# A two-layer encoder trunk: the last group of w_down, too, by seven block products

## The chip, the cores and the metric

The kernel runs on one core of a Trainium2 chip. The metric is the device time of one execution in microseconds (us). Before the change it is 2019.84 us, the median of 3 runs (2019.82 to 2021.61). One execution was recorded by the hardware profiler; its own time is 2019.96 us.

A core has a matrix engine (TensorE, PE in the profile, its weight loads PEld), a vector engine (VectorE, DVE), a scalar engine (ScalarE, ACT), GpSimd (POOL) and SyncE (SP), which issues nearly all loads here. Each engine runs its own list of instructions in order and waits on semaphores for the others.

## The reference

Two layers over 256 tokens of width 2048, all in float32. Each layer is a normalisation, a mixing part (three kinds of attention and an output projection), another normalisation and a feed-forward part that is 8192 wide. The change touches only the second product of the feed-forward part:

```python
h = rmsnorm(x, norm_mlp[l])
u = jax.nn.relu(jnp.einsum('bsd,df->bsf', h, w_up[l]))
x = x + jnp.einsum('bsf,fd->bsd', u * u, w_down[l])
...
return rmsnorm(x, norm_final)
```

## The kernel before

**Precision.** Every float32 operand of a matmul is kept as two parts in a shorter format: a high part (`whi`, a ScalarE cast) and the rest (`wlo`, a VectorE subtraction, `TENSOR_TENSOR` on L989). The helper `split` (L978) makes both for one weight tile of 128x1024. A product takes three matmuls instead of one: high by high, low by high and high by low. The activations `uT` carry both parts from the start.

**Steps.** The program is a list of steps (`steps`), one weight tile each. While step i runs, loads are issued for six steps ahead (L964), the split of step i + 2 is made and preparations of step i + 4 (`prep`). The tiles whi and wlo rotate through three buffers each, so the split of a step waits until the step three places ahead of it has used its own. A scheduler turns this list into an order for each engine.

**The feed-forward part** is cut into eight groups g of 1024 hidden columns. Group g has 16 *up steps* (`up_steps`, L691 and L696: 8 matmuls of 512 columns and 8 of 256), which make four tiles uT of 256 hidden columns each, and it has its share of w_down, 1024 rows by 2048 columns. The four column chunks j of 512 are taken in two ways:

- *Plain steps* (`down_steps`, matmuls on L477): for a chunk, 4 steps of 12 matmuls add up in two PSUM banks, one for each half of the tokens, and VectorE adds the banks to the residual x (L739).
- *Product steps* (`strassen_steps`, L802): chunks 0 and 1 of groups 0 to 6 are seen as 2x2 block matrices and computed with seven block products instead of eight. They go by the names P1, P6, P7, P5, P3, P2, P4, in this order. A product is two steps (h = 0 and 1) of 6 matmuls. The weight sums that the products need (B12 + B11 and so on) are made by VectorE over 128x1024 (`prep`, L815 to L832); the sums of activation blocks are made once for each uT tile (`sums_of`, L712 to L717). P1, P6, P5 and P3 add up in one bank, P7 and P4 in a second one, both in the tile S; P2 has its own. Behind each product VectorE adds the bank to x (L782). The next product that writes S waits for that.

The quarters of w_down are B11, B12, B22 and B21, each in two halves. B11 lies in the tiles `spare`, the others in `side`, of which there are four; B21's halves come last and take the places of B12's, once P7's splits have read those.

**The order** is written out by hand. With group g's products go group g's plain steps for chunks 2 and 3 and the up steps of group g + 1:

```python
for g in range(7):
    ss = down_steps(g, (2, 3)) + up_steps(g + 1)
    hs = strassen_steps(g)
    order = [0, 0]
    for p_ in range(7):
        order += [1, 0, 1] + ([0, 0] + [0] * (p_ in (1, 3, 5)) if p_ < 6 else [])
steps.extend(down_steps(7, range(4)))
```

A 1 is a product step, a 0 the next of the others. Between two products stand two or three other steps. Group 7 is four plain chunks, 16 steps, and behind each chunk `layer_end` starts the next layer's transposes of that chunk (`hprep`), or in the last layer the squares for the final normalisation (`final_chunk`).

Of the kernel before, what the change touches and what calls it, by code (L numbers as in the profile page):

```python
# [23 lines left out]
P = 128  # L24
# [19 lines left out]
def tile_trunk(ctx: ExitStack, tc: tile.TileContext, x_in, w_in, w_o, w_up, w_down,  # L44
# [459 lines left out]
    def layer_steps(l):  # L504
# [152 lines left out]
        def up_steps(g):  # L657

            out_, evacs = [], []
            for q in range(4 * g, 4 * g + 4):  # L660
                box = {}

                def evac(q=q, box=box):
# [14 lines left out]
                    if q < 28:  # L678
                        sums_of(q, a)
# [40 lines left out]
        def down_steps(g, js):  # L720
            out_ = []
            for j in js:
                box = {}
                for k in range(4):
                    def mm(wh, wl, j=j, k=k, box=box):
                        if k == 0:
                            box["b"] = [mm_bank(), mm_bank()]
                            box["w"] = []
                        final = l == L - 1 and g == 7 and j == 3
                        hts = [uT[4 * g + k]] * 2  # L730
                        mode_b(box["b"], hts, wh, wl, [0, 1], k == 0, k == 3, blocks=(0,) if final else (0, 1),
                               lo_last=g < 7)
                        box["w"].append((hts, wh, wl))
                        if k < 3:
                            return

                        def evac(t):
                            xs = x[:, t, j * 512:(j + 1) * 512]
                            nc.vector.tensor_add(xs, xs, box["b"][t])  # L739
                        if final:  # L740
                            evac(0)
                            final_block(0)
                            tail = [mm_bank(), mm_bank()]
                            for c in range(2):
                                cols = slice(c * 256, c * 256 + 256)
                                for i, (hts, vh, vl) in enumerate(box["w"]):
                                    mode_b([None, tail[c]], hts, vh[:, :, cols], vl[:, :, cols], [0, 1],
                                           i == 0, i == 3, n=256, blocks=(1,))
                                xs = x[:, 1, 1536 + c * 256:1792 + c * 256]
                                nc.vector.tensor_add(xs, xs, tail[c][:, 0:256])  # L750
                                square_cols(1, 1536 + c * 256, 256, fin["ss"][:, 7 + c:8 + c])
                            final_block(1)
                            return
# [421 lines left out]
```

## Time and profile before

| | |
|---|---|
| median of 3 runs | 2019.84 us |
| profiled execution, its own time | 2019.96 us |
| its span, first to last instruction | 2018.2 us |
| TensorE busy | 2003.0 us (99%) |
| VectorE busy | 1644.0 us (81%) |
| ScalarE busy | 1208.2 us (60%) |
| group 6 of the second layer | about 1880.8 to 1966.3 us |
| group 7 of the second layer, plain | 1966.3 us to the end of its matmuls |

Rows of the timeline give start, length, engine, line, operation, the tile written and the tiles read, the shape and a count; a bracket at the end is the engine's idle time before the row and what ended it. A matmul's length overlaps the next one, so times are taken from start to start. Rows of windows give a stretch, its length and each engine's busy time.

### The profile page before, as it was taken

The numbers are of one execution on the slowest core, as the hardware profiler recorded it, in microseconds if no ns is written. First come the engines' busy times: TensorE is split into PE (matmuls) and PEld (weight loads), VectorE is DVE, ScalarE is ACT, GpSimd is POOL, SyncE is SP. The second block draws the span as 40 slices with busy tenths as digits, with TensorE's granted clock in tenths as the row PEclk, the third lists the DMA queues.
The fourth block names the chain that finished last, engine by engine and source line by source line (L and its number), as shares of the span: only waits on it lengthen the run. The fifth ranks groups of instructions, "written<-read, shape, count | busy, mean of one in ns | idle before, by whom it ended". The sixth has DMA issues, their size and how long they took to land.

```text
span 2018.2 us, 27873 instructions
## 1 busy us (share of the span) xinstructions
PE 2003.0 (99%) x10264; PEld 1707.6 (85%) x10264; DVE 1644.0 (81%) x2095; ACT 1208.2 (60%) x1748; POOL 257.2 (13%) x296
## 2 busy tenths in 40 slices
PE   9999999999999999999999999999999999999998
PEld 7888788888888888888888888888888888888887
DVE  6777977879888898887658789778888888888975
ACT  6667756565555556555656676565655556565554
POOL 0493330000000000000005744200000000000001
PEclk9999999999999999999999999999999999999999
DMA  8655465566565756656656455565665756657554
GB/s 279 197 167 154 165 190 188 175 212 191 184 222 171 223 186 190 213 173 199 188 179 185 156 165 175 180 188 181 194 210 174 231 167 209 203 170 235 165 166 156
DMA packets 108821, 381.28 MB, mean 189 GB/s; under 512 B 12259, under 2 KB 16611, under 8 KB 108684
## 3 DMA queue, kind: packets, MB, share of 16 engines
q1 hardware_dynamic: 108252, 378.41, 59.0%
q8 instruction: 80, 1.31, 0.2%
q10 hardware_dynamic: 432, 1.10, 0.1%
q14 instruction: 57, 0.47, 0.1%
HBM read 377.34 MB, written 2.11 MB: 188 GB/s over the span
## 4 chain that ended last, share of the span: by engine, by line
PE 93%; DVE 3%; ACT 1%; POOL 1%; issue 1%; DMA 1%; SPq 0%; DVEq 0%; POOLq 0%
PE mm L477 40%; PE mm L691 23%; PE mm L696 12%; PE S L802 11%; PE mm L802 2%; PE tr L392 1%; PE tr L219 1%; POOL big L939 1%; DVE wlo L989 1%; PE tr L411 1%; ACT big L372 1%; DVE big L287 1%; PE S L351 1%; PE S L350 1%; DVE big L394 0%
## 5 line engine op out<-in xcount | busy, mean ns | idle before, releaser
L988 ACT CAST whi<-wraw 128x1024 fp32r<-128x1024 f32 (+1 forms) x531 | 556.9, 1051 | 421.9 <-PE mm L691 170.2
L989 DVE TENSOR_TENSOR wlo<-wraw,whi 128x1024 fp32r<-128x1024 f32 (+1 forms) x531 | 655.9, 1237 | 184.7 <-ACT whi L988 181.8
L477 PE MATMUL mm<-whi,big 128*128 128x512 f32 (+1 forms) x2252 | 643.8, 386 | 0.3 <-ACT whi L988 0.3
L691 PE MATMUL mm<-big,whi 128*128 128x512 f32 x2048 | 509.6, 391 | 0.0
L477 PEld LDWEIGHTS mm<-whi,big 128*128 128x128 f32 x2252 | 419.0, 188 | 82.9 <-ACT whi L988 2.3
L691 PEld LDWEIGHTS mm<-big,whi 128*128 128x128 f32 x2048 | 377.4, 188 | 73.7
L477 PE MATMUL mm<-wlo,big 128*128 128x512 f32 (+1 forms) x1126 | 375.7, 385 | 1.0 <-DVE wlo L989 1.0
L696 PEld LDWEIGHTS mm<-big,wlo 128*128 128x128 f32 x2048 | 279.5, 191 | 19.9
L696 PE MATMUL mm<-big,wlo 128*128 128x256 f32 x2048 | 285.7, 283 | 0.0
L477 PEld LDWEIGHTS mm<-wlo,big 128*128 128x128 f32 x1126 | 212.0, 188 | 41.8 <-DVE wlo L989 2.3
L802 PE MATMUL S<-whi,big 128*128 128x512 f32 x672 | 182.3, 393 | 0.0
L477 PE MATMUL mm<-spare,big 128*128 128x512 f32 (+1 forms) x678 | 158.5, 382 | 0.0
L988 ACT CAST whi<-side 128x1024 fp32r<-128x1024 f32 x84 | 88.3, 1051 | 95.5 <-PE mm L691 78.0
L477 PEld LDWEIGHTS mm<-spare,big 128*128 128x128 f32 x678 | 122.3, 188 | 23.1
L802 PEld LDWEIGHTS S<-whi,big 128*128 128x128 f32 x672 | 119.2, 189 | 18.6
L989 DVE TENSOR_TENSOR wlo<-side,whi 128x1024 fp32r<-128x1024 f32 x84 | 102.6, 1222 | 37.2 <-ACT whi L988 36.9
L383 POOL TENSOR_SCALAR big<-big,sm 128x256 f32<-128x256 f32 x128 | 89.4, 716 | 247.0 <-DVE sm L381 208.9
L255 POOL TENSOR_TENSOR sm<-sm,mhalf 128x2 f32<-128x2 f32 (+2 forms) x14 | 13.4, 954 | 793.5 <-DVE sm L250 773.6
L988 ACT CAST whi<-big 128x1024 fp32r<-128x1024 f32 x56 | 58.9, 1052 | 85.3 <-DVE big L817 36.4
L802 PE MATMUL S<-wlo,big 128*128 128x512 f32 x336 | 104.0, 391 | 0.0
L870 POOL TENSOR_TENSOR x<-x,big 128x512 f32<-128x512 f32 x6 | 8.6, 1456 | 669.5 <-ACT mid L877 669.5
L988 ACT CAST whi<-spare 128x1024 fp32r<-128x1024 f32 x56 | 59.0, 1053 | 47.8 <-PE mm L691 27.8
(152 smaller groups left out, 2093.8 us busy)
## 6 DMA issues: line engine op xcount, KB each, us to landing
wraw<-in_w_up_dram SPq DMA_DIRECT2D x256, 512.0 KB, 4.2
wraw<-in_w_down_dram SPq DMA_DIRECT2D x144, 512.0 KB, 3.7
wraw<-in_w_in_dram SPq DMA_DIRECT2D x119, 512.0 KB, 3.8
side<-in_w_down_dram SPq DMA_DIRECT2D x84, 512.0 KB, 4.3
wraw<-in_w_o_dram SPq DMA_DIRECT2D x64, 512.0 KB, 3.9
spare<-in_w_down_dram SPq DMA_DIRECT2D x28, 512.0 KB, 4.3
side<-in_rpb_dram SPq DMA_DIRECT2D x32, 174.8 KB, 5.0
side<-avec SPq DMA_DIRECT2D x8, 384.0 KB, 5.2
```

Of the source, the lines that this page charges most:

```text
L219: tr = nc.tensor.transpose(psv[:, kk, t, :], x[:, t, c0:c0 + P], ident).ins
L287: nc.vector.tensor_sub(kl[rows, par::2, :], z, f(kh[rows, par::2, :]))
L350: nc.tensor.matmul(o, st, u.kh[:, kh, :], start=True, stop=False)
L351: nc.tensor.matmul(o, st, u.kl[:, kh, :], start=False, stop=True)
L372: nc.scalar.activation(p[:, s, :], src[s], AF.Exp, bias=negm[:, s:s + 1], scale=u.rq[:, s:s + 1] if u.kind == "C" else 1.0, accum_out=sums ...
L383: nc.gpsimd.tensor_scalar(p[:, s, :], p[:, s, :], rs[:, s:s + 1], 1.0, op0=ALU.mult, op1=ALU.mult)
L477: return nc.tensor.matmul(banks[t][:, 0:n], a, (wl if part == "hl" else wh)[:, i, :], start=first and i == 0 and part == "hh", stop=last a ...
L691: nc.tensor.matmul(box["b"][fs], wh[:, kk, fs * P:(fs + 1) * P], ht, start=s == 0 and kk == 0, stop=False, skip_group_check=True)
L696: nc.tensor.matmul(box["b"][fs][:, 0:256], wl[:, kk, fs * P:(fs + 1) * P], ht[:, 0:256], start=False, stop=s == 3 and kk == 3, skip_group_ ...
L802: nc.tensor.matmul(o, ops[i][a], w[:, i, :], skip_group_check=True, start=fresh and h == 0 and i == 0 and a == 0 and w is wh, stop=h == 1 ...
L988: act = nc.scalar.copy(h[:, part], w[:, part]).ins
L989: last_lo[0] = nc.vector.tensor_sub(lo[:, part], w[:, part], f(h[:, part])).ins
```

## The change

The last group's chunks 0 and 1 are taken by the seven products as well. The plain steps that are left are put elsewhere: group 6's products have only the 16 up steps of group 7 between them, and group 7's products get group 6's plain chunks. Chunk 2 of groups 6 and 7 is added up in one go, 8 steps on the same two banks; chunk 3 of group 6 follows, and group 7's chunk 3 comes last, as before. `layer_end` now comes for chunk 1 behind P3, for chunk 2 behind its eight steps, for chunk 0 behind P4, and for chunk 3 at the end. `sums_of` runs for all 32 tiles, and the weights of group 7 are packed like the others.

```diff
-                    if q < 28:
-                        sums_of(q, a)
+                    sums_of(q, a)
...
-        def down_steps(g, js):
+        def down_steps(gs, j):
+            out_, box = [], {}
+            tiles = [(g, k) for g in gs for k in range(4)]
+            final = l == L - 1 and gs == (7,)
+            for n, (g, k) in enumerate(tiles):
+                def mm(wh, wl, g=g, k=k, n=n):
+                    last = n == len(tiles) - 1
...
+                    mode_b(box["b"], hts, wh, wl, [0, 1], n == 0, last, blocks=(0,) if final else (0, 1),
+                           lo_last=gs != (7,))
...
+                    if gs[-1] == 7:
+                        layer_end(l, j)
+                out_.append(Step(w_down[l, (g * 4 + j) * 4 + k], 2, 512, None, mm, fourth=gs == (7,)))
...
                         if h == 1:
                             evac(o, *dst)
+                            if g == 7 and name in ("P3", "P4"):
+                                layer_end(l, dst[1])
...
-        for g in range(7):
-            ss = down_steps(g, (2, 3)) + up_steps(g + 1)
+        for g in range(8):
+            if g < 6:
+                ss = down_steps((g,), 2) + down_steps((g,), 3) + up_steps(g + 1)
+            elif g == 6:
+                ss = up_steps(7)
+            else:
+                ss = down_steps((6, 7), 2) + down_steps((6,), 3) + down_steps((7,), 3)
             hs = strassen_steps(g)
             order = [0, 0]
             for p_ in range(7):
-                order += [1, 0, 1] + ([0, 0] + [0] * (p_ in (1, 3, 5)) if p_ < 6 else [])
+                order += [1, 0, 1]
+                if p_ < 6:
+                    order += [0] * (2 if g < 6 else g == 6) + [0] * (g != 6 and p_ in (1, 3, 5))
+            order += [0] * (len(ss) - order.count(0))
-        steps.extend(down_steps(7, range(4)))
...
-    if g < 7:
-        b = w.reshape(8, P, D)
+    b = w.reshape(8, P, D)
```

Lines behind the first hunk move by a few: the product matmuls stand on L803, the splits on L1000 (cast) and L1001, the evacuation of a product on L783, the weight sums on L819 to L836.

**Group 6 of the second layer, VectorE,** from the split of P6's second half to the evacuation of P6. The names in the rows: `wlo<-big` the split of P6 (it reads the sum in `big`), `wlo<-wraw` that of an up or plain step, `wlo<-side` of P7, `side<-side,side` the weight sum for P7, `x<-x,S` the evacuation. Before:

```order
L989 TENSOR_TENSOR wlo_17672<-big_17635,whi_17671 128x1024 [waits PE_49,Activation_49]
L989 TENSOR_TENSOR wlo_17684<-wraw_17615,whi_17683 128x1024 [waits DMAHW3_49,PE_49,Activation_49]
L989 TENSOR_TENSOR wlo_17700<-wraw_17628,whi_17699 128x1024 [waits DMAHW4_49,PE_49,Activation_49]
L821 TENSOR_TENSOR side_17559<-side_17559,side_17561 128x1024
L782 TENSOR_TENSOR x<-x,S_17585 128x512 [waits PE_49]
```

And in the change:

```order
L1001 TENSOR_TENSOR wlo_17728<-big_17679,whi_17727 128x1024 [waits Activation_49]
L670 SCALAR_TENSOR_TENSOR mid_17710<-mid_17710,rrow 128x512 [waits DVE_49]
L825 TENSOR_TENSOR side_17586<-side_17586,side_17588 128x1024
L711 TENSOR_TENSOR mid_17720<-mid_17710 128x256 [waits Activation_49]
L676 TENSOR_TENSOR big_17717<-mid_17710,big_17717 128x512 [waits Activation_49]
L712 SCALAR_TENSOR_TENSOR mid_17720<-mid_17720,mid_17710 128x128 [waits DVE_49]
L1001 TENSOR_TENSOR wlo_17741<-wraw_17652,whi_17740 128x1024 [waits DMAHW2_49,PE_49]
L713 SCALAR_TENSOR_TENSOR mid_17720<-mid_17720,mid_17710 128x128 [waits DVE_49]
L1001 TENSOR_TENSOR wlo_17763<-side_17586,whi_17762 128x1024 [waits PE_49,Activation_49]
L716 TENSOR_TENSOR big_17724<-mid_17720,big_17724 128x512 [waits Activation_49]
L825 TENSOR_TENSOR side_17634<-side_17634,side_17636 128x1024
L783 TENSOR_TENSOR x<-x,S_17645 128x512 [waits PE_49]
```

The evacuation and the block sums of a finished uT tile now stand between P6's split and its evacuation, since an up step comes at every second place.

**P1 into P6, TensorE.** Before, in group 6 (the end of P1, then the first of two plain steps):

```order
L802 MATMUL S_17585<-wlo_17582,big_17384 128x512 [waits DVE_49]
L802 MATMUL S_17585<-wlo_17582,big_17516 128x512
L477 MATMUL mm_17545<-whi_17596,big_17516 128x512 [waits Activation_49]
L477 MATMUL mm_17545<-whi_17596,big_17516 128x512
L477 MATMUL mm_17546<-whi_17596,big_17516 128x512 x2
```

In the change, in group 7 of the second layer:

```order
L803 MATMUL S_18240<-wlo_18237,big_18021 128x512 [waits DVE_49]
L803 MATMUL S_18240<-wlo_18237,big_18181 128x512
L803 MATMUL S_18240<-whi_18247,big_17724 128x512 [waits DVE_49,Activation_49]
L803 MATMUL S_18240<-whi_18247,big_17875 128x512
L803 MATMUL S_18240<-whi_18247,big_17724 128x512
L803 MATMUL S_18240<-whi_18247,big_17875 128x512
L477 MATMUL mm_18197<-whi_18268,big_17563 128x512 [waits Activation_49]
```

P6's first matmul stands right behind P1's last one and waits for VectorE.

**The same place on VectorE.** From the split of P1's second half on, in the change:

```order
L1001 TENSOR_TENSOR wlo_18237<-spare_18137,whi_18236 128x1024 [waits DMAHW6_49,PE_49]
L713 SCALAR_TENSOR_TENSOR mid_18184<-mid_18184,mid_18174 128x128 [waits DVE_49]
L819 TENSOR_TENSOR spare_18137<-spare_18137,side_18211 128x1024 [waits DMAHW4_49,DVE_49]
L716 TENSOR_TENSOR big_18188<-mid_18184,big_18188 128x512 [waits Activation_49]
L821 TENSOR_TENSOR big_18220<-side_18152,spare_18103 128x1024
L821 TENSOR_TENSOR big_18252<-side_18213,spare_18137 128x1024 [waits DMAHW6_49,DVE_49]
L783 TENSOR_TENSOR x<-x,S_18240 128x512 [waits PE_49]
L1001 TENSOR_TENSOR wlo_18248<-big_18220,whi_18247 128x1024 [waits Activation_49]
```

Three weight sums and two instructions of the last uT tile stand between the split and the evacuation of P1 (L783), for which P6 waits.

More of the change, by code (lines that the diff above doesn't have):

```diff
@@ L718, in sums_of @@
             sT[q] = t
-        def down_steps(g, js):
[L721 to L732, printed above, removed]
-                        box["w"].append((hts, wh, wl))
[L734 to L753, printed above, removed]
-                        evac(0)
-                        evac(1)
-                        if g == 7:
-                            layer_end(l, j)
-                    out_.append(Step(w_down[l, (g * 4 + j) * 4 + k], 2, 512, None, mm, fourth=g == 7))
@@ L1110, in _pack_down @@
     plain = [_pack(w[:, j * 512:(j + 1) * 512], 2) for j in range(4)]
-    if g < 7:
-        b = w.reshape(8, P, D)
-        plain[0:2] = [np.stack([b[[4 * h + par, 4 * h + par + 2], :, j * 512:(j + 1) * 512].transpose(1, 0, 2).reshape(P, 1024)
-                                for j in range(2) for h in range(2)]) for par in range(2)]
+    b = w.reshape(8, P, D)
+    plain[0:2] = [np.stack([b[[4 * h + par, 4 * h + par + 2], :, j * 512:(j + 1) * 512].transpose(1, 0, 2).reshape(P, 1024)
+                            for j in range(2) for h in range(2)]) for par in range(2)]
     return np.concatenate(plain)
```

25 lines of the change are left out of this document (added).

## The prediction

> **What bounds the kernel now.** I read the page's busy times first, then what TensorE waited for, then the end of the second layer in stretches.
>
> ```profile
> span 2018.2 us, 27873 instructions
> ...
> PE 2003.0 (99%) x10264; PEld 1707.6 (85%) x10264; DVE 1644.0 (81%) x2095; ACT 1208.2 (60%) x1748; POOL 257.2 (13%) x296
> ```
>
> ```profile
> PE tr L392 <- DVE big L287: 2.6, 2, 1.3
> ...
> PE mm L477 <- DVE wlo L989: 1.0, 2, 0.5
> ```
>
> ```profile
> 1880.80:1911.00 30.20, 30.20 (x138) 25.19 (x138) 29.47 (x35) 16.17 (x17) 0.00 (x0) 1.00 0.52 168
> 1911.00:1966.30 55.30, 55.30 (x300) 47.99 (x299) 41.50 (x44) 32.28 (x41) 0.00 (x0) 1.00 0.54 164
> 1966.30:2003.00 36.70, 36.70 (x163) 30.41 (x162) 23.53 (x25) 18.98 (x27) 7.73 (x6) 1.00 0.51 170
> ```
>
> TensorE is the bound: busy 99%, and its longest waits are two of 1.3 us in the attention. The stretches (length, then busy us of PE, PEld, DVE, ACT, POOL, then granted clock) are the first third of group 6, its rest, and group 7. TensorE has no idle time in any. But VectorE is busy 29.47 of 30.20 us in the first and 23.53 of 36.70 us in group 7. So fewer matmuls shorten the run only where VectorE can follow, and the first third of a group is where it has nothing left.
>
> **What is removed.** TensorE's timeline (start, length, line, count; I take times from start to start):
>
> ```profile
> 1876.68 1.98 PE L691 MATMUL mm<-big,whi 128*128 128x512 f32 x8
> 1878.50 1.12 PE L696 MATMUL mm<-big,wlo 128*128 128x256 f32 x8
> 1879.45 1.09 PE L802 MATMUL S<-whi,big 128*128 128x512 f32 x4
> ...
> 1880.84 1.98 PE L477 MATMUL mm<-whi,big 128*128 128x512 f32 x8
> ...
> 1886.28 1.07 PE L802 MATMUL S<-whi,big 128*128 128x512 f32 x4
> ...
> 1887.64 1.98 PE L477 MATMUL mm<-whi,big 128*128 128x512 f32 x8
> ...
> 1890.36 1.07 PE L802 MATMUL S<-whi,big 128*128 128x512 f32 x4
> ```
>
> An up step takes 1879.45 - 1876.68 = 2.77 us (1.82 with whi, 0.95 with wlo), a plain step 1890.36 - 1887.64 = 2.72 (0.227 a matmul), a product step 1.36 behind a plain step and 1880.84 - 1879.45 = 1.39 behind an up step. In each layer 8 plain steps (21.76 us) become 14 product steps (14 x 1.36 = 19.04): 12 matmuls and 2.72 us less, 5.44 in two layers. If nothing waited, the profiled 2019.96 us (span 2018.2 and 1.8 around it) would be 2014.5.
>
> **What is added** lies on VectorE, 31 instructions a layer: 6 splits, 8 sums of weight blocks, 4 instructions for the block sums of each of the four last u tiles, and 7 evacuations where there were 4 for columns 0 and 1 and 2 more for group 6's own column chunk 2. Its prices, and where it stands as group 6 begins:
>
> ```profile
> 1879.78 1.23 DVE L989 TENSOR_TENSOR wlo<-wraw,whi 128x1024 fp32r<-128x1024 f32 x1 [1.04 <-ACT whi L988]
> 1880.92 0.74 DVE L669 TENSOR_TENSOR mid<-mid,mm 128x256 f32<-128x256 f32 x2
> 1881.58 0.68 DVE L782 TENSOR_TENSOR x<-x,S 128x512 f32<-128x512 f32 x1
> 1882.18 0.69 DVE L670 SCALAR_TENSOR_TENSOR mid<-mid,rrow 128x512 f32<-128x512 f32 x1
> 1882.78 1.22 DVE L989 TENSOR_TENSOR wlo<-spare,whi 128x1024 fp32r<-128x1024 f32 x1
> 1883.94 1.23 DVE L989 TENSOR_TENSOR wlo<-wraw,whi 128x1024 fp32r<-128x1024 f32 x1
> 1885.21 0.69 DVE L676 TENSOR_TENSOR big<-mid,big 128x512 fp32r<-128x512 f32 x1
> 1885.82 0.42 DVE L712 TENSOR_TENSOR mid<-mid 128x256 f32<-128x256 f32 x1
> 1886.16 1.22 DVE L815 TENSOR_TENSOR spare<-spare,side 128x1024 f32<-128x1024 f32 x1
> 1887.29 0.28 DVE L713 SCALAR_TENSOR_TENSOR mid<-mid,mid 128x128 f32<-128x128 f32 x1
> 1887.50 1.22 DVE L989 TENSOR_TENSOR wlo<-spare,whi 128x1024 fp32r<-128x1024 f32 x1
> ```
>
> Start to start, a split or a sum over 128x1024 takes 1.14 us (1879.78 to 1880.92; 1.13 to 1.16 elsewhere), 512 columns 0.60, 256 columns 0.34, 128 columns 0.21; L676 began 0.13 late. That is 14 x 1.14 + 0.60 + 4 x (0.34 + 2 x 0.21 + 0.60) = 22 us a layer, hidden behind TensorE as long as VectorE is ahead. ScalarE gets 10 casts more, but it is busy 32.28 of 55.30 us. SP issues as many loads as before. The changed order shows where VectorE is late: two places in each layer, and one more that hangs on a load.
>
> **Place 1, first third of group 6.** The plain steps that lay here are gone, so TensorE meets the products sooner: four times up step and product, 4.16 us, in which VectorE has two splits (2.28) and its share of sums and evacuations. Let t = 0 be the end of the previous group's last product. An up step and a product lie ahead of it as before, so VectorE starts as in the trace, 1880.84 - 1879.78 = 1.06 us before. From there the order gives it, up to and with the split of the up step behind P6's second half, 14 instructions of 1.14, 7 of 0.60, 6 of 0.34 and 3 of 0.21: 22.83 us, two late starts of 0.13, and 0.08 to the end of the last: done at t = 22.1. TensorE wants that split after 5 up steps, 4 products and 1.82: 13.85 + 5.56 + 1.82 = 21.2. It waits 0.9. Then P7 stands behind 0.95 + 1.82 more, at t = 24.9, and must wait until P6's sum is out of the two-bank tile S. In VectorE's order that comes after a block sum (0.21), a split, a 512-column step and a weight sum: 22.0 + 0.21 + 1.14 + 0.60 + 1.14 = 25.1, and 0.68 more, 25.8. It waits 0.9 again. **Taken: 1.8**; with 17 wide instructions at 1.13 and no late start 1.3, at 1.16 and two more late starts 2.4. The low end stays above zero: a gain is excluded: VectorE has no idle to take work into.
>
> **Place 2, P1 into P6 of group 7.** No plain step stands between them any more, and P6 adds to the bank that VectorE must first empty. How a release reaches the other engine:
>
> ```profile
> 202.69 1.22 DVE L989 TENSOR_TENSOR wlo<-wraw,whi 128x1024 fp32r<-128x1024 f32 x1
> ...
> 203.07 0.39 PE L477 MATMUL mm<-whi,big 128*128 128x512 f32 x1
> ...
> 203.96 0.50 PE L477 MATMUL mm<-wlo,big 128*128 128x512 f32 x1 [0.49 <-DVE wlo L989]
> ```
>
> The matmul starts 203.96 - 203.91 = 0.05 us behind VectorE's end, and a matmul lasts 0.39, 0.16 longer than its 0.227 of the stream. So even a VectorE that is on time costs 0.16 + 0.05 + 0.68 + 0.05 = 0.94 us, where the plain steps had covered it. Is it on time? Let T be the end of the layer's last up step. The split of P1's first half takes that step's whi buffer (three rotate); in the trace such a split (1879.78) started 3.10 after the up step that frees it (1876.68), so here at T + 0.33, and it lets go at T + 1.47. Ahead of the evacuation the order then has 7 wide instructions, 3 of 512, 3 of 256 and 2 of 128 columns: 7.98 + 1.80 + 1.02 + 0.42 = 11.22, with two late starts T + 12.95. With 0.68 and 0.05, P6 starts at T + 13.7. TensorE is there after two plain steps, a product, a plain step and a product: 3 x 2.72 + 2 x 1.36 = T + 10.9. **Taken: 2.75**; bounds 0.94 (on time) and 3.1 (wide ones at 1.16, two more late starts). It is nearest the upper rows, since nothing in that list can go elsewhere.
>
> **Place 3, P7 into P5 of group 7.** The order puts most of a plain step between them, but ahead of P7's evacuation VectorE has to add the two halves of B21 to P4's weights, and these halves take side buffers that only P7's splits free. The same in group 6 now:
>
> ```profile
> 1906.99 0.33 SPq L968 DMA_DIRECT2D side<-in_w_down_dram  x1
> ...
> 1914.14 0.33 SPq L968 DMA_DIRECT2D side<-in_w_down_dram  x1
> ```
>
> ```profile
> 1911.76 1.23 DVE L832 TENSOR_TENSOR big<-side,big 128x1024 f32<-128x1024 f32 x1 [1.32 <-DMA side<-in_w_down_dram]
> ...
> 1917.62 1.23 DVE L832 TENSOR_TENSOR big<-side,big 128x1024 f32<-128x1024 f32 x1 [1.10 <-DMA side<-in_w_down_dram]
> ```
>
> From issue to use 4.77 and 3.48 us. Let u be P6's start. Five splits on, the fifth of them P7's first, VectorE is at u + 5.8, and a weight sum, an evacuation and two splits later, the last of them P7's second, at u + 9.8; there the two loads are issued. The first sum starts at u + 5.8 + 4.77 = u + 10.6, and with it and two splits VectorE is free again at u + 14.0. With 3.48 the second sum starts then and P5 may start 1.14 + 0.68 + 0.05 later, at u + 15.9; with 4.77 at u + 16.4. TensorE arrives at 4.08 + 2 x (1.36 + 2.72) + 1.36 + 2.26 = u + 15.9. **Taken: 0.35**, bounds 0 and 0.6. Behind the waiting sum stand two splits and the evacuation, which is why it matters.
>
> Elsewhere I cost the change at nothing: the four plain steps at each layer's end (10.9 us) hide the last evacuation and the next layer's transposes of chunk 0, and work behind the last matmul is as it was.
>
> **Sum:** -2.72 + 1.8 + 2.75 + 0.35 = +2.2 us a layer, +4.4 in all: 2024.4 for the profiled run, **2024.3 us** against the median of 2019.84. With all low bounds but place 2 at 2.3 it is +0.9 a layer, with all high ones +3.4: 2021.6 to 2026.6.
>
> **Rivals.** *VectorE is on time* (not slower): place 1 and 3 cost nothing, place 2 its 0.94, -1.78 a layer, 2016.3; it decides at place 2, if the evacuation starts before T + 11.1 rather than T + 12.95. For it speaks that VectorE's 81% leaves room on average, against it the 29.47 of 30.20. With no stall at all 2014.4. *The B21 loads are late*: with 1.2 us more than 4.77 (the difference of the two rows shown, once more) place 3 costs 1.8, +1.45 a layer more, 2027.2; group 7 issues its loads in a shorter time, but TensorE's steps there are no denser than in group 6's first third, where the loads were not late. *The array slows after the longer idle times*: place 2's wait is twice the longest in the middle of this trace. The start of the run shows what a slow array costs:
>
> ```profile
> 1.61 2.92 PE L999 MATMUL mm<-warm 128*128 128x512 f32 x6 [1.61 <-DVE warm L996]
> ...
> 5.28 1.50 PE L1012 MATMUL mm<-warm 128*128 128x512 f32 x4
> ```
>
> (2.92 - 0.39) / 5 = 0.51 us a matmul, then (1.50 - 0.39) / 3 = 0.37: six at 0.28 more and four at 0.14 are 2.2 us, in two layers 4.5, 2028.8. Against it stands a stretch around the later of the two 1.3 us waits, where TensorE was busy 2.64 of 4 us and the granted clock stayed at 1.00:
>
> ```profile
> 1230.00:1234.00 4.00, 2.64 (x19) 2.01 (x18) 3.90 (x8) 3.67 (x10) 1.68 (x4) 1.00 0.22 89
> ```
>
> The Trainium skill (TensorE: Matmul & The Clock Gate, "HAM oscillation — how this bites in real kernels") puts the gap that throttles at about 3.4 us; by that rule 2.75 costs no clock, and no run here shows a longer gap. It also says (PSUM — Partial Sum Buffer, "PSUM bank collisions raise a hardware error") that a guard by bank and quadrant is enough. P7 and P6, P5 and P7 lie in different banks, so by it two of the waits need not be; the sum would then be -2.72 + 0.9 + 2.75, about 2021.7. The program waits by the whole tile, and I go by the program.
>
> **How the numbers follow.** Forecast 0.68, VectorE on time or nearly 0.16, late loads 0.11, slow array 0.05. About 0.2% (4 us, what a measurement here can tell from no change) over 2019.84 is 2023.9; of the forecast's 0.68 some 0.42 lie above it, since its middle is close to that line. Slower 0.42 + 0.16 = 0.58; faster (below 2015.8) 0.04, the no-stall end; the same 0.38. The range takes half of the on-time case and most of the late loads: 2018.0 to 2028.0; the forecast's own is 2021.6 to 2026.6.
>
> **What would show it.** 24 matmuls fewer and TensorE's busy time down by about 5.4. New rows in TensorE's waits: L803 for x L783, some 0.9, 2.7 and 0.3 us in each layer, L695 for wlo L1001 some 0.9. The longest wait ends at P6 of group 7; VectorE runs without idle from the last product of group 5 to P7 of group 6. Wrong it is if TensorE's waits in groups 6 and 7 sum to under 2.7 us a layer, or if the clock row drops.

## The result and the profile after

| | before | changed |
|---|---|---|
| median | 2020.14 us (6 runs, 2019.82 to 2021.61) | 2027.74 us (6 runs, 2026.66 to 2029.03) |
| profiled execution, own time | 2019.96 us | 2026.89 us |
| span | 2018.2 us | 2025.1 us |

The ratio is 1.0038, with a 95% interval of 1.0026 to 1.0049: 7.6 us slower. The forecast of 2024.3 had the direction, but only a little more than half of the size. The result lies within the stated 2018.0 to 2028.0, but above the forecast's own range, which ends at 2026.6.

The page of the changed kernel, span and busy times:

```profile
span 2025.1 us, 27936 instructions
...
PE 2000.9 (99%) x10240; PEld 1701.0 (84%) x10240; DVE 1686.5 (83%) x2157; ACT 1224.3 (60%) x1768; POOL 258.1 (13%) x296
```

The 24 matmuls are gone (10264 to 10240) and VectorE is 42.5 us busier. What TensorE waited for (total us, times, longest):

```profile
PE S L803 <- DVE x L783: 7.0, 6, 2.7
...
PE mm L477 <- DVE wlo L1001: 1.7, 3, 0.7
...
PE mm L695 <- DVE wlo L1001: 1.3, 2, 0.6
```

In the kernel before the first and the third of these rows are not there at all, and the second stood at 1.0 in two waits. TensorE's timeline of the second layer, at the places of the prediction (the idle time and its releaser stand in brackets):

```profile
1902.79 1.98 PE L690 MATMUL mm<-big,whi 128*128 128x512 f32 x8
1905.40 1.21 PE L695 MATMUL mm<-big,wlo 128*128 128x256 f32 x8 [0.63 <-DVE wlo L1001]
1906.45 2.00 PE L690 MATMUL mm<-big,whi 128*128 128x512 f32 x8
1909.07 1.20 PE L803 MATMUL S<-whi,big 128*128 128x512 f32 x4 [0.62 <-DVE x L783]
...
1959.35 0.61 PE L803 MATMUL S<-wlo,big 128*128 128x512 f32 x2
1962.63 1.17 PE L803 MATMUL S<-whi,big 128*128 128x512 f32 x4 [2.67 <-DVE x L783]
...
1978.17 0.39 PE L477 MATMUL mm<-wlo,big 128*128 128x512 f32 x1
1979.08 1.20 PE L803 MATMUL S<-whi,big 128*128 128x512 f32 x4 [0.53 <-DVE x L783]
...
2006.96 0.51 PE L477 MATMUL mm<-wlo,big 128*128 128x512 f32 x1 [0.67 <-DVE wlo L1001]
```

A wait costs the idle time plus 0.16, by which the matmul ahead of it outlasts its slot of 0.227. From start to start, place 1 lost 1905.40 - 1902.79 - 1.81 = 0.80 and 1909.07 - 1906.45 - 1.84 = 0.78, place 2 1962.63 - 1959.35 - 0.45 = 2.83, place 3 1979.08 - 1978.17 - 0.23 = 0.68. About 0.1 more goes behind each of them, where the first matmuls come a little apart. In the first layer the same sums give 0.80, 0.78, 2.55 and 0.37. VectorE ahead of places 2 and 3:

```profile
1959.53 2.36 DVE L821 TENSOR_TENSOR big<-side,spare 128x1024 f32<-128x1024 f32 x2
1961.80 0.68 DVE L783 TENSOR_TENSOR x<-x,S 128x512 f32<-128x512 f32 x1
...
1977.20 1.23 DVE L836 TENSOR_TENSOR big<-side,big 128x1024 f32<-128x1024 f32 x1 [0.60 <-DMA side<-in_w_down_dram]
1978.35 0.68 DVE L783 TENSOR_TENSOR x<-x,S 128x512 f32<-128x512 f32 x1
```

Each evacuation (L783) ends 0.05 to 0.15 us before the matmul that waits for it, and the one at place 3 stands behind a sum that waited for a load. These are the predicted waits, at the predicted instructions. Two things are new.

**The end.** The last row is a wait that the prediction did not have. The last four plain steps of the second layer, from their first matmul to the first of the 256-column tail, in the kernel before and then in the changed one:

```profile
1998.97 0.39 PE L477 MATMUL mm<-whi,big 128*128 128x512 f32 x1
...
2004.41 0.28 PE L477 MATMUL mm<-whi,big 128*128 128x256 f32 x1
```

```profile
2004.37 0.39 PE L477 MATMUL mm<-whi,big 128*128 128x512 f32 x1
...
2011.32 0.28 PE L477 MATMUL mm<-whi,big 128*128 128x256 f32 x1
```

5.44 us before, 6.95 after: 1.51 lost. VectorE and GpSimd in the changed kernel just ahead:

```profile
1989.84 2.14 DVE L1001 TENSOR_TENSOR wlo<-wraw,whi 128x1024 fp32r<-128x1024 f32 x1
...
1995.11 2.09 DVE L1001 TENSOR_TENSOR wlo<-wraw,whi 128x1024 fp32r<-128x1024 f32 x1 [1.40 <-ACT whi L1000]
```

```profile
1986.70 4.19 POOL L882 TENSOR_TENSOR x<-x,big 128x512 f32<-128x512 f32 x2 [658.35 <-ACT mid L889]
1993.50 2.61 POOL L882 TENSOR_TENSOR x<-x,big 128x512 f32<-128x512 f32 x2 [2.61 <-ACT mid L889]
```

Splits that take 1.22 elsewhere take 2.1 where they overlap GpSimd's multiplications of x by the final norm's gains.

**The executions differ.** The granted clock is the share of its full clock that TensorE is given. Three executions took 2026.66 to 2027.04 us at a mean granted clock of 0.999, three 2028.43 to 2029.03 at 0.998; the median lies in the gap between the two groups. The kernel before was at 0.999 every time. The profiled execution is one of the first three. The others have no profile; profiles of the experiments show what lowers the clock.

For the profiled execution the terms add up: -5.44 for the matmuls, in two layers +3.6 at place 1, +5.5 at place 2, +1.3 at place 3 (each with the 0.1 behind it), and +1.5 at the end: +6.5. The span grew by 6.9; 0.4 us is not assigned.

### The profile page after: what moved, and what is told of

Same layout as the page of the kernel before. It is cut to its first block, busy times and chain, and to the rows that moved or that the text cites. A ratio compares the mean times of both kernels' runs of the same rounds, so it can differ in the third digit from the quotient of the medians.

```text
span 2025.1 us, 27936 instructions
## 1 busy us (share of the span) xinstructions
PE 2000.9 (99%) x10240; PEld 1701.0 (84%) x10240; DVE 1686.5 (83%) x2157; ACT 1224.3 (60%) x1768; POOL 258.1 (13%) x296
## 5 line engine op out<-in xcount | busy, mean ns | idle before, releaser
L1000 ACT CAST whi<-wraw 128x1024 fp32r<-128x1024 f32 (+1 forms) x521 | 546.4, 1051 | 389.8 <-PE mm L690 154.4
L1001 DVE TENSOR_TENSOR wlo<-wraw,whi 128x1024 fp32r<-128x1024 f32 (+1 forms) x521 | 644.2, 1239 | 156.0 <-ACT whi L1000 150.4
L477 PE MATMUL mm<-whi,big 128*128 128x512 f32 (+1 forms) x2172 | 614.1, 386 | 0.3 <-ACT whi L1000 0.3
L477 PEld LDWEIGHTS mm<-whi,big 128*128 128x128 f32 x2172 | 403.5, 188 | 80.4 <-ACT whi L1000 2.5
L477 PE MATMUL mm<-wlo,big 128*128 128x512 f32 (+1 forms) x1086 | 356.7, 385 | 1.8 <-DVE wlo L1001 1.7
L695 PEld LDWEIGHTS mm<-big,wlo 128*128 128x128 f32 x2048 | 279.2, 190 | 22.0 <-DVE wlo L1001 2.1
L695 PE MATMUL mm<-big,wlo 128*128 128x256 f32 x2048 | 285.7, 282 | 1.3 <-DVE wlo L1001 1.3
L477 PEld LDWEIGHTS mm<-wlo,big 128*128 128x128 f32 x1086 | 204.3, 188 | 42.2 <-DVE wlo L1001 4.2
L803 PE MATMUL S<-whi,big 128*128 128x512 f32 x768 | 208.8, 393 | 7.0 <-DVE x L783 7.0
L1000 ACT CAST whi<-side 128x1024 fp32r<-128x1024 f32 x96 | 100.9, 1051 | 104.5 <-PE mm L690 70.5
L803 PEld LDWEIGHTS S<-whi,big 128*128 128x128 f32 x768 | 136.2, 189 | 31.1 <-ACT whi L1000 5.8
L1001 DVE TENSOR_TENSOR wlo<-side,whi 128x1024 fp32r<-128x1024 f32 x96 | 117.5, 1224 | 33.1 <-ACT whi L1000 32.6
L477 PE MATMUL mm<-spare,big 128*128 128x512 f32 (+1 forms) x606 | 141.1, 381 | 0.0
L477 PEld LDWEIGHTS mm<-spare,big 128*128 128x128 f32 x606 | 108.7, 188 | 20.3
L1000 ACT CAST whi<-big 128x1024 fp32r<-128x1024 f32 x64 | 67.3, 1052 | 89.3 <-DVE big L821 41.2
L803 PE MATMUL S<-wlo,big 128*128 128x512 f32 x384 | 118.7, 390 | 0.0
L1000 ACT CAST whi<-spare 128x1024 fp32r<-128x1024 f32 x64 | 67.4, 1053 | 50.8 <-PE mm L690 30.2
```

The source lines that it names most:

```text
L477: return nc.tensor.matmul(banks[t][:, 0:n], a, (wl if part == "hl" else wh)[:, i, :], start=first and i == 0 and part == "hh", stop=last a ...
L695: nc.tensor.matmul(box["b"][fs][:, 0:256], wl[:, kk, fs * P:(fs + 1) * P], ht[:, 0:256], start=False, stop=s == 3 and kk == 3, skip_group_ ...
L803: nc.tensor.matmul(o, ops[i][a], w[:, i, :], skip_group_check=True, start=fresh and h == 0 and i == 0 and a == 0 and w is wh, stop=h == 1 ...
L1000: act = nc.scalar.copy(h[:, part], w[:, part]).ins
L1001: last_lo[0] = nc.vector.tensor_sub(lo[:, part], w[:, part], f(h[:, part])).ins
```

## Experiments

In what follows theory A is that of the prediction: VectorE is late at certain places, TensorE waits there, and VectorE has time elsewhere. Theory B is that VectorE's total work in groups 6 and 7 sets the end. All kernels start from the changed one. Each ratio is to the kernel before, run beside them: its median was 2020.14 us beside the changed kernel, 2019.83 beside the next four and 2020.36 beside the others. The last column counts executions by their mean granted clock.

| kernel | median us | range | ratio to before | executions with clock below 0.999 |
|---|---|---|---|---|
| changed | 2027.74 | 2026.66 to 2029.03 | 1.0026 to 1.0049 | 3 of 6 |
| plain step behind P1, P6, P7, P5 | 2028.42 | 2025.72 to 2029.99 | 1.0028 to 1.0053 | 4 of 5 |
| own bank | 2026.88 | 2025.50 to 2027.05 | 1.0021 to 1.0046 | 6 of 6 |
| fewer sums | 2020.35 | 2020.06 to 2020.93 | 0.9994 to 1.0011 | 0 of 11 |
| no gains on GpSimd | 2027.16 | 2026.74 to 2028.53 | 1.0024 to 1.0049 | 5 of 5 |
| plain step added ahead of P6 | 2022.77 | 2022.28 to 2022.96 | 1.0003 to 1.0021 | 0 of 11 |
| filled wait | 2023.83 | 2023.49 to 2024.47 | 1.0009 to 1.0027 | 0 of 11 |
| shorter wait | 2024.08 | 2023.80 to 2025.95 | 1.0011 to 1.0029 | 0 of 11 |
| two plain steps in group 6 | 2028.72 | 2027.12 to 2029.51 | 1.0026 to 1.0053 | 5 of 5 |
| spread | 2017.64 | 2017.34 to 2018.28 | 0.9979 to 0.9996 | 0 of 11 |
| spread, gains at the end | 2016.46 | 2016.29 to 2016.65 | 0.9972 to 0.9989 | 0 of 11 |

### A plain step behind each of four products

```diff
-            order = [0, 0]
+            order = [0, 0] if g < 7 else [0]
...
-                    order += [0] * (2 if g < 6 else g == 6) + [0] * (g != 6 and p_ in (1, 3, 5))
+                    order += [0] * (2 if g < 6 else 1 if g == 6 else p_ < 4) + [0] * (g < 6 and p_ in (1, 3, 5))
```

> The changed kernel, with the plain steps of group 7 in another order: one of them stands behind each of P1, P6, P7 and P5, one fewer ahead of P1, none behind P3 and P2. Nothing else differs. Theory A (hand-overs: TensorE waits at P6 and P5 of group 7 because nothing stands between a product and the next one that uses its bank): a plain step of 2.72 us covers each hand-over, so the waits of 2.55 and 2.83 at P6 and of 0.37 and 0.69 at P5 in the changed kernel's two layers go down to 0.3 or less, 5.5 to 6.8 us less, 2021 to 2022.3. Theory B (VectorE has no time to give in groups 6 and 7: what its instructions sum to sets the end, and a wait that is covered shows up again further on): less than 2 us, 2026 or more.

Measured: 2028.42 us, no gain. Theory A as it was put here, that a bare hand-over between neighbours is the cost, fell. TensorE's waits and VectorE around P6 of group 7 in the first layer:

```profile
PE S L803 <- ACT whi L1000: 5.0, 2, 2.6
```

```profile
954.21 0.68 DVE L783 TENSOR_TENSOR x<-x,S 128x512 f32<-128x512 f32 x1
...
956.75 2.36 DVE L821 TENSOR_TENSOR big<-side,spare 128x1024 f32<-128x1024 f32 x2
```

The evacuation of P1 now comes early, at 954.21, but P6 still waits 2.4 and 2.6 us, for the cast of its weights. The block sums those are made of (L821) run from 956.75 on, the first ready at 957.97; a cast takes 1.05, and P6 starts at 959.15. So the neighbourhood is not what counts: the plain step behind P1 was taken from ahead of P1, TensorE comes to P6 after the same work as before, and VectorE has as much to do up to there. The wait at P5 went from 0.37 and 0.68 to under 0.1.

The windows show the second thing: the stretch with the wait at P6, the one behind it and the next, in the first layer, then the first two of these in the second layer (length, PE, PEld, DVE, ACT, POOL, granted clock):

```profile
955.91:959.32 3.41, 0.99 (x5) 0.53 (x4) 3.38 (x5) 1.26 (x2) 0.00 (x0) 1.00 0.00 0
959.32:962.73 3.41, 3.41 (x9) 2.65 (x10) 3.31 (x3) 2.72 (x3) 0.00 (x0) 0.50 0.13 18
962.73:966.15 3.42, 3.42 (x17) 2.81 (x16) 2.04 (x2) 1.14 (x2) 0.00 (x0) 1.00 0.57 168
1959.43:1962.84 3.41, 1.43 (x7) 0.85 (x5) 3.41 (x4) 1.11 (x2) 0.00 (x0) 1.00 0.74 293
1962.84:1966.25 3.41, 2.82 (x7) 2.25 (x8) 3.38 (x4) 3.14 (x4) 0.00 (x0) 0.50 0.02 5
```

In the third stretch TensorE works on 17 matmuls, in the second, at half clock, on 9. Eight matmuls at 0.43 us instead of 0.227 cost 8 x 0.2 = 1.6 us; in the second layer, where the clock fell before the wait was over, it is 1.3.

The changed kernel's profiled execution has waits of the same length and no half clock. Its windows at P6, two in the first layer and two in the second:

```profile
954.70:958.12 3.42, 2.22 (x10) 1.50 (x8) 3.42 (x4) 1.11 (x2) 0.00 (x0) 1.00 0.00 0
958.12:961.53 3.41, 2.23 (x10) 1.87 (x11) 3.41 (x5) 3.36 (x4) 0.00 (x0) 1.00 0.00 0
...
1958.22:1961.64 3.42, 1.74 (x8) 1.12 (x6) 3.42 (x4) 1.11 (x2) 0.00 (x0) 1.00 0.53 216
1961.64:1965.05 3.41, 2.42 (x11) 2.01 (x12) 3.41 (x5) 3.20 (x4) 0.00 (x0) 1.00 0.02 5
```

These windows are not chosen freely. In each of the twelve traces the granted clock changes only on one grid of 3.413 us, and the windows are steps of that grid. Seven steps at half clock lie at P6, in four traces; ahead of each is a step in which TensorE was busy for only 0.75 to 1.43 us. No step with 1.59 us or more has half clock behind it. So by the traces it is the place of the wait on the grid that decides: in the changed kernel's profiled execution a grid line cuts each wait into pieces of 1.7 us and less, and enough work is left in every step.

### An own bank for P7 and P4

```diff
                             box["a"], box["d"] = pair[:, 0], pair[:, 1]
+                        if (name, h) == ("P7", 0) and g >= 6:
+                            box["d"] = mm_bank()
```

> The changed kernel, with the second bank of the block products (that of P7 and P4) a tile of its own in groups 6 and 7 rather than half of the tile S. P7 then waits for no evacuation of P6, and P5 for none of P7. Theory A: the waits of 0.78 us at P7 of group 6 and of 0.37 and 0.69 at P5 of group 7, each with 0.1 behind it, go: 3 us less, 2024.7. Theory B (VectorE is late in any case): TensorE goes on by one step and then waits for the next split by as much; less than 1 us, 2026.7 or more.

Measured: 2026.88 us; the profiled execution, 2025.50 with one stretch at half clock (in the second layer), against 2026.89 without one.

```profile
PE S L805 <- DVE x L783: 5.0, 2, 2.7
...
PE mm L805 <- ACT whi L1002: 1.3, 2, 0.7
```

The waits for an evacuation fall from six to two, those at place 2. P5 waits no longer: place 3 was the tile's tracking and nothing else. In group 6, L695's wait is gone from the list, but P7 still waits 0.7, now for its weights; start to start 0.82 is left of 1.58. So theory A holds for place 3 and theory B for half of place 1: there VectorE was late whatever the bank. By the rows, about 3 us are saved; the medians show 0.9, since all six executions here had stretches at half clock. For the profiled execution it adds up: 2026.89 - 3 + 1.6 for its one stretch is 2025.5.

### Fewer sums ahead of P6

```diff
                         def prep(h=h):
+                            if g == 7:
+                                return
                             nc.vector.tensor_add(raw["B11", h], raw["B11", h], raw["B12", h])
...
-                        get = lambda h=h: t2[h]
+                        get = lambda h=h: raw["B11", h] if g == 7 else t2[h]
```

> The changed kernel, without the four sums of weight blocks ahead of P6 in group 7 (P6 multiplies B11 alone and P4 B11 + B21, so the output is another). VectorE has 4 x 1.14 = 4.6 us less to do in each layer, all of it ahead of its evacuation of P1. Theory A (P6 waits because VectorE is late with that evacuation): it is then on time and the wait at P6 shrinks from 2.55 and 2.83 us to the bare hand-over of 0.94 that the prediction worked out; the wait at P5, which hangs on the loads of B21, stays. 3.5 us less, 2024.2. Theory B (the sum of VectorE's work sets the end): up to 9 us less, 2019. Theory C (the hand-over through the bank costs this much however early VectorE is): no change, 2027.7.

Measured: 2020.35 us, 7.4 less. TensorE in the first layer:

```profile
956.35 0.61 PE L803 MATMUL S<-wlo,big 128*128 128x512 f32 x2
956.80 1.07 PE L477 MATMUL mm<-whi,big 128*128 128x512 f32 x4
957.75 1.19 PE L803 MATMUL S<-whi,big 128*128 128x512 f32 x4
```

Place 2 is gone, 0.04 left in both layers. Theory C falls with it. The bare hand-over of 0.94 does not appear as a wait either, but it is there: TensorE's order now has four matmuls of the next plain step (0.91 us) between P1 and P6, and P6 starts 957.75 - 956.80 = 0.95 after the first of them. Of the 7.4 us, 5.3 are the two waits at P6 and 0.6 those at P5, some 0.8 of the changed kernel's median are half clock, which no execution has here, and 0.7 is not assigned (the profiled execution, from which the rows come, took 0.6 more than its kernel's median). By the number alone, 2020.35 is nearer to theory B's 2019 than to theory A's 2024.2. The rows speak against B: of 9.1 us of VectorE work, what was saved is what was waited for, and the waits of place 1 stay. Theory A's number was too high because it left the hand-over of 0.94 uncovered and the wait at P5 unchanged.

### No gains on GpSimd

```diff
-            nc.gpsimd.tensor_mul(xs, xs, fin["g"][j // 2][:, (j % 2) * 512:(j % 2) * 512 + 512])
```

> The changed kernel, without GpSimd's multiplication of columns 0 to 1535 of x by the last norm's gains in the second layer's end (so the output lacks them). In the changed kernel three of VectorE's splits that run beside these multiplications take 2.14, 2.09 and 1.55 us instead of 1.22, and TensorE loses 1.5 us in the last four plain steps, 0.84 of it waiting for a split. Theory A (the multiplications hold up VectorE): without them these splits take 1.22, and the loss at the end goes down to 0.4 or less; 1.1 to 1.5 us less, 2026.4. Theory B (the last four plain steps are too short, since each does only the first token block, and VectorE would be late without the multiplications too): no change at the end, 2027.7.

Measured: 2027.16 us, within the scatter of the changed kernel, since all five executions had stretches at half clock (the profiled one two). The rows decide. The same splits and the wait list:

```profile
1992.96 1.23 DVE L1000 TENSOR_TENSOR wlo<-wraw,whi 128x1024 fp32r<-128x1024 f32 x1 [0.32 <-ACT whi L999]
...
1997.32 1.23 DVE L1000 TENSOR_TENSOR wlo<-wraw,whi 128x1024 fp32r<-128x1024 f32 x1 [1.36 <-ACT whi L999]
```

```profile
PE mm L477 <- DVE wlo L1000: 1.0, 2, 0.5
```

The splits take 1.23 again, and L477 waits as in the kernel before (1.0, two times): nothing is lost in the last four steps. Theory A holds for the end.

### One more plain step ahead of P6

```diff
-                    order += [0] * (2 if g < 6 else g == 6) + [0] * (g != 6 and p_ in (1, 3, 5))
+                    order += [0] * (2 if g < 6 else g == 6) + [0] * (g != 6 and p_ in ((1, 3, 5) if g < 6 else (0, 3, 5)))
```

> The changed kernel, with one plain step of group 7 moved from between P6 and P7 to between P1 and P6; unlike in the run that set plain steps behind P1, P6, P7 and P5, both plain steps ahead of P1 stay. VectorE has the same count of wide instructions ahead of its evacuation of P1 (a split in the place of a sum). Theory A (VectorE's queue up to P6, counted from the layer's last up step, against what TensorE has to do up to there): TensorE comes to P6 2.72 us later and VectorE no later, so the wait of 2.55 and 2.83 us goes, with it the slower matmuls that sometimes follow, and P5, which then starts later against its loads, waits no longer either; P7 now stands right behind P6 and may wait 0.3 to 0.9. 2020.5 to 2022. Theory B (the sum of VectorE's work in groups 6 and 7 sets the end): the wait comes back in another place, 2025 or more.

Measured: 2022.77 us (2022.28 to 2022.96), 0.8 above the expected range.

```profile
PE S L803 <- DVE x L783: 1.2, 2, 0.6
```

Only the waits at P7 of group 6 are left in this row; places 2 and 3 are gone but for 0.1. The expectation missed the end: about 2.1 us are lost in the last plain steps instead of 1.5. Together with the first experiment this settles what place 2 is: what counts is how much of TensorE's work stands ahead of P6 since VectorE was last free, not what stands next to it.

### The wait filled with matmuls

This starts from the kernel with the own bank, in which every execution had a stretch at half clock, by the mean clock.

```diff
+                        if (name, h) == ("P6", 0) and g == 7:
+                            idle = mm_bank()
+                            for _ in range(8):
+                                nc.tensor.matmul(idle, warm[:, 0:P], warm, start=True, stop=True)
                         o = box[bk]
```

> The kernel with the own bank for P7 and P4, with eight matmuls of the start's warm tile (result unused) put ahead of P6 in group 7: 1.8 us of TensorE's wait of 2.55 and 2.83 us is then work, and P6 can start no sooner. In the runs before, matmuls right behind this wait took 0.43 us instead of 0.227 for some 3.4 us (granted clock 0.50 to 0.54) in one or in both layers; the kernel with the own bank had one such stretch in its executions of 2025.5 and two, by the mean clock, in those of 2027.0. Theory A (the clock drops because TensorE is idle): no such stretch in any execution, the idle time at P6 is 0.8 to 1.0, all executions near 2023.8. Theory B (the matmuls are slow for another reason, such as the operands or what the other engines do then): the stretches stay, 2025.5 to 2027.

Measured: 2023.83 us, the expected number; no execution of 11 below 0.999. TensorE in the second layer, and the window from 1960.00 on:

```profile
1957.40 2.00 PE L804 MATMUL mm<-warm 128*128 128x512 f32 x8
1960.23 1.16 PE L809 MATMUL S<-whi,big 128*128 128x512 f32 x4 [0.83 <-DVE x L783]
```

```profile
1960.00:1963.40 3.40, 3.17 (x14) 2.65 (x15) 3.40 (x4) 2.44 (x3) 0.00 (x0) 1.00 0.06 12
```

Sixteen matmuls of no use make the kernel 3 us faster than the one with the own bank. Idle time of TensorE is what halves the clock.

### A shorter wait

```diff
-                            nc.vector.tensor_add(raw["B11", h], raw["B11", h], raw["B12", h])
+                            n = 256 if g == 7 and h == 1 else 512
+                            nc.vector.tensor_add(raw["B11", h][:, :, 0:n], raw["B11", h][:, :, 0:n], raw["B12", h][:, :, 0:n])
```

> The changed kernel, with one of the four sums of weight blocks ahead of P6 in group 7 made over half of its columns (so the output is another): VectorE's queue is about 0.55 us shorter, and the wait at P6 of group 7 goes from 2.55 and 2.83 us down to about 2.0 and 2.3. Theory A (the clock drops by how long TensorE is idle, with a limit between the 1.3 us waits of the kernel before, after which it never dropped, and 2.55): fewer stretches of slow matmuls than in the changed kernel (three of six executions); each execution without one near 2025.7. Theory B (the limit lies below 2 us): as many or more, 2027.4.

Measured: 2024.08 us, 0 of 11 below 0.999.

```profile
PE mm L477 <- ACT whi L1001: 3.0, 2, 1.5
```

The wait is shorter than expected, 1.5 us idle, because TensorE's order changed too: the next plain step stands ahead of P6 and waits. So waits of 1.5 us, two in each of 11 executions if they are like the profiled one, never halved the clock; in the profiled execution they left 2.06 and 1.91 us of work in the grid step of 3.41 us. In the kernels with idle times of 2.4 us and more at P6, two in each execution, 23 of 27 executions had it at least once, by the mean clock.

### Two plain steps in group 6's first third

The order of group 6 begins with two plain steps of its own chunk 3 (e) in the place of two up steps (u); P is a product step, c a step of chunk 2 of both groups, f the last four.

```diff
...
+        for g, order in ((6, "eePuPuPuPuPuPuPuPuPuPuPuPuPuuu"),
+                         (7, "ccPcPPcPcPcPPcPcPPPePPePffff")):
```

> The changed kernel, with two of the four plain steps of group 6's own column chunk 3 put ahead of group 6's P1 (two up steps go behind its P4 instead), so group 7 has two fewer between its last products. Ahead of P1, P6 and P7 of group 7 all stays. Theory A (VectorE has too little time in group 6's first third, and each plain step there gives it 2.72 - 1.14 us): the waits of 0.80 and 0.78 us there go down to 0.2 or less in sum, 1.5 a layer; the waits at P6 and P5 of group 7, counted from the layer's last up step, stay as they are (2.55 to 2.9, 0.4 to 0.8). An execution without slow matmuls 2024, the median with some of them 2024 to 2026. Theory B (VectorE is one long queue from group 5 to P6 of group 7): what TensorE no longer waits in group 6 it waits at P6 of group 7, that wait grows to 4 us, 2026.5 or more.

Measured: 2028.72 us, no gain; both stretches at half clock are in the profiled execution.

```profile
PE S L803 <- DVE x L783: 5.8, 4, 2.4
PE mm L477 <- DVE wlo L998: 2.9, 4, 1.2
```

Place 1 is gone in both layers; the four waits in the first row are those of places 2 and 3, which did not grow (2.54 and 2.55, 0.6 and 0.8 from start to start). So theory A holds here, and the debt of group 6 isn't carried to group 7. The time was lost elsewhere: two plain steps fewer between group 7's last products brought the wait at the end to 1.2 and 0.7 us, and all five executions had stretches at half clock.

### The steps spread

The same steps in one order that gives VectorE time at all three places (it ran before the kernel above):

```diff
...
+        for g, order in ((6, "euPuPuPePuuuPPuPPuuPuuPuPPuuPuP"),
+                         (7, "ueccPcPePcPcPPPcPcPPPPPcPffff")):
```

> The changed kernel with the same steps in another order in groups 6 and 7: two of the four plain steps of group 6's own column chunk 3 lie in group 6's first third and the other two at the start of group 7, up steps stand in front of the products of group 6's second half, and plain steps stand behind P1, P6 and P7 of group 7. The number of each kind of instruction is that of the changed kernel. Theory A (VectorE is late only in places, and has time elsewhere): no wait above 0.4 us in groups 6 and 7, 2.72 us a layer less than before, less up to 0.7 of small waits: 2015 to 2016.5, faster than both. Theory B (VectorE's sum sets the end): 2020 or more.

Measured: 2017.64 us, ratio 0.9987 (0.9979 to 0.9996): faster than both kernels, though 1.1 us above the expected range. In TensorE's waits no row of L803 or L695 is left; places 1 to 3 are gone, and 0.22 a layer is lost at P7 of group 7, which now follows P6 with one plain step between. What the expectation missed is again the end:

```profile
1991.15 1.72 DVE L998 TENSOR_TENSOR wlo<-big,whi 128x1024 fp32r<-128x1024 f32 x1
1992.80 2.31 DVE L998 TENSOR_TENSOR wlo<-wraw,whi 128x1024 fp32r<-128x1024 f32 x1
```

So one more, with less for GpSimd to do there:

```diff
-            nc.gpsimd.tensor_mul(xs, xs, fin["g"][j // 2][:, (j % 2) * 512:(j % 2) * 512 + 512])
+            if j == 2:
+                nc.gpsimd.tensor_mul(xs, xs, fin["g"][1][:, 0:512])
...
-        nc.vector.tensor_scalar(x[:, t, 0:1024], x[:, t, 0:1024], r, None, op0=ALU.mult)
+        xs = x[:, t, 0:1024]
+        nc.vector.scalar_tensor_tensor(xs, xs, r, fin["g"][0], op0=ALU.mult, op1=ALU.mult)
```

> The kernel with the steps spread over groups 6 and 7, with the last norm's gains for columns 0 to 1023 multiplied by VectorE in the two closing instructions that scale by the row's factor (one of 1024 columns each) instead of by GpSimd beforehand; GpSimd keeps columns 1024 to 1535. Theory A (VectorE's splits lose 0.5 to 1.1 us each beside a GpSimd multiplication, and with that TensorE loses 1.3 us in the last four plain steps): the loss there goes to 0.3 or less, the closing instruction behind the last matmul takes 1.4 instead of 0.75, net 0.4 to 0.7 less, 2017. Theory B (the last four steps are too short for VectorE in any case): the loss stays and the end is 0.7 longer, 2018.3.

Measured: 2016.46 us, ratio 0.9981 (0.9972 to 0.9989), 3.9 us faster than the kernel before. The same two splits, and the closing instruction:

```profile
1991.07 1.22 DVE L1000 TENSOR_TENSOR wlo<-big,whi 128x1024 fp32r<-128x1024 f32 x1
1992.21 1.22 DVE L1000 TENSOR_TENSOR wlo<-wraw,whi 128x1024 fp32r<-128x1024 f32 x1
...
2009.46 1.28 DVE L904 SCALAR_TENSOR_TENSOR x<-x,sm,big 128x1024 f32<-128x1024 f32 x1
```

## Why the prediction was right in direction and short in size

**What is removed: right.** 24 matmuls are gone. TensorE's busy time fell by 2.1 us, not 5.4: each wait leaves a last matmul shown at 0.39 instead of its 0.227, and the first ones behind a wait come a little apart, so busy time is no measure of the saving. The last experiment bears the 5.44 out: it keeps 3.9 of them, and its remaining losses that the rows show are two times 0.22, 0.7 in the last plain steps (a split of 2.26 us beside the multiplication that GpSimd kept) and 0.5 for the longer closing instruction.

**Place 1: right.** 0.9 and 0.9 were predicted; 0.80 and 0.78 and the 0.1 behind each were measured, in both layers. From the end of group 5's last product (1883.38) on, the waiting L695 came at 22.0 us where 22.1 was predicted, and P7 at 25.7 for 25.8; the rows show no idle time of VectorE up to there. The reason holds: plain steps there, in the place of up steps, remove both waits.

**Place 2: right in size (2.75 against 2.55 and 2.83), half right in its reason.** The arithmetic of VectorE's queue from the last up step's end (1948.89) on was borne out: the evacuation starts 12.91 us behind it, for 12.95, and P6 13.74, for 13.7. But it named the evacuation of P1 as what P6 waits for. The first experiment had that evacuation done 4 us ahead of P6, and P6 waited as long for its own weights, whose sums stand in the same queue. In the changed kernel their cast had ended only 0.6 us ahead of the evacuation (1961.88 against 1962.48).

**Place 3: right in its reason, small in size.** 0.35, with bounds 0 and 0.6, against 0.37 and 0.68 with 0.1 behind each. P5 waits because the evacuation of P7 stands in VectorE's queue behind sums that wait for B21's loads; with a bank of its own it does not wait.

**"Elsewhere I cost the change at nothing": wrong, and the larger miss.** The step counted 10.9 us for the four plain steps at each layer's end. In the second layer these do only the first token block ahead of the tail, 5.44 us by the rows of the kernel before, and VectorE arrives there late, since two of its splits lose 0.9 us each beside GpSimd. That is 1.5 us, and without GpSimd's multiplications it is nothing. In the kernel before the same overlap was there, but among 16 plain steps VectorE had time for it (its timeline, with the idle time that follows):

```profile
1981.26 1.95 DVE L989 TENSOR_TENSOR wlo<-wraw,whi 128x1024 fp32r<-128x1024 f32 x1 [1.54 <-ACT whi L988]
1983.98 1.23 DVE L989 TENSOR_TENSOR wlo<-wraw,whi 128x1024 fp32r<-128x1024 f32 x1 [0.77 <-ACT whi L988]
```

**The rival of the slow array: set aside wrongly.** It got a chance of 0.05, on the ground of a 1.3 us wait after which the clock stayed at 1.00. For a wait twice as long that was no evidence. In half of the executions, by their time and mean clock, one wait at P6 was followed by 3.4 us at half clock, 1.6 us each. A falling clock was one of the prediction's own signs of being wrong. The forecast of +4.4 thus lacks 1.5 at the end, 0.6 at place 3 with what follows the waits, 0.4 that is not assigned and, in the median, some 0.8 for the clock: 7.7, against the measured 7.6.

The Trainium skill (TensorE: Matmul & The Clock Gate, "HAM oscillation — how this bites in real kernels"), by whose 3.4 us the prediction let the wait pass, does not agree with these runs: 2.4 to 2.7 us idle were enough in most executions, 1.5 us in none. The same page ("What's actually happening") describes an activity window of about 3.4 us that runs freely. The length of the slow stretch here, 3.41 us, and the grid of 3.413 us on which the clock changes agree with it, and by the windows shown with the first experiment the place of the wait on that grid is why the same wait is followed by half clock in one execution and not in another. No run moved a wait along the grid on purpose.

Its other rule in the prediction (PSUM — Partial Sum Buffer, "PSUM bank collisions raise a hardware error"), that a guard by bank is enough, was borne out at place 3; in group 6 0.82 of the 1.58 us stayed, because VectorE was late there in any case.

**The range: luck in part.** Its upper end of 2028.0 was set by late loads, which did not come: place 3 lost 0.7 at most in the profiled execution. What filled the room was the end and the clock, of which one was put at nothing and the other at a chance of 0.05.

## What to carry to other kernels

Where an engine is busy 81% on average but full in some stretches, fewer instructions on the bound engine make the stretches denser: add up the other engine's queue from the last point at which it was free, stretch by stretch, and put work of the bound engine ahead of the place where the queue is longest, not next to it. Look at the last steps of the program by themselves, since a tail that does half the work in a step gives half the cover. And count a wait of TensorE above 2 us or so as longer than it looks (here the clock fell when 2.0 us or more of one grid step of 3.41 were idle); matmuls of no use that fill it can be worth their place until the wait itself is removed.

## What the runs showed of the hardware

- After TensorE had been idle for 2.4 to 2.7 us, its granted clock could fall to half (0.50) for 3.41 us (a 512-column matmul took 0.43 us from start to start instead of 0.227). By the mean clock it happened in 23 of 27 executions of the five kernels with such waits, and in none of 66 of the six kernels whose longest wait there was 1.5 us or less. Filling 1.8 us of the wait with matmuls ended it.
- In twelve traces the granted clock changed only on a grid of 3.413 us. It fell behind every grid step with TensorE busy for 1.43 us or less, and behind none with 1.59 us or more.
- A VectorE subtraction over 128x1024 took up to 2.3 us instead of 1.22 while GpSimd multiplied 128x512 tiles, and two of GpSimd's took 4.19 us together there (1.36 one alone).
